# Merge gates and branch products of a hybrid decoder block computed with their columns over the partitions

## The chip, the cores and the metric

The kernel runs on one core of a Trainium2 chip. The time is that of one execution on the device, in microseconds (us). The engines are named as in the profile: PE is the matrix engine TensorE, PEld its weight loads, DVE is VectorE, ACT is ScalarE, POOL is GpSimd and SP is SyncE, which issues nearly all transfers from device memory.

## The reference

One decoder block, 256 tokens (S) of 2048 features (D), float32. Two token mixers work on projections of the same normalised input. Each result is gated and projected by its own branch matrix; the two branch products are merged by sigmoid gates, and the merged matrix is projected out.

```python
proj = h @ w_in                                     # 2048 x 11824
(qa, kc, vc, ks, vs, kw, vw, ga, za, qb, kb, vb, zb, ma, mb) = jnp.split(proj, IN_SPLITS, axis=-1)
...
ya = (oa * jax.nn.silu(za.astype(F32))).astype(x.dtype) @ w_br_a      # 1024 x 2048
yb = (ob * jax.nn.silu(zb.astype(F32))).astype(x.dtype) @ w_br_b      # 1024 x 2048
merged = jax.nn.sigmoid(ma) * ya + jax.nn.sigmoid(mb) * yb
out = merged @ w_out                                                  # 2048 x 2048
return x + (gate[:, None, :] * rms_norm(out, g_post)).astype(x.dtype)
```

`ma`, `mb`, `ya`, `yb` and `merged` are 256 x 2048. `gate`, like the scale and shift inside `h`, is a third of `c @ w_ada + b_ada`, a product of one row.

## The kernel before, in words

**Weights.** Every weight matrix is read once, in tiles of 1024 columns per partition (`raw`, seven buffers): for the large products two blocks of 128 rows by a panel of 512 columns. `prep` (L473) splits a tile into two parts: ACT rounds it to `wH` (L477), and DVE subtracts to get the rest, `wL` (L479). For the branch and output products POOL takes every fourth item of the list instead of DVE, where that item is a weight tile (L478). There are three buffers each for `wH` and `wL`, and conversion runs three items ahead of the products. The activations are split in the same way (`xH`, `xL`; `yH`, `yL`; `mH`, `mL`), and a product is the sum of three: H x H, L x H and H x L.

**Products.** `product` (L518) has two forms. In the ordinary one the activations are the stationary operand, 128 tokens of them, and 512 weight columns move (L535, L536 with `wH`, L538 with `wL`): the result has tokens over the partitions, `job.ps[t]` is the token half t. In the other one (`job.turned`) 128 weight columns are stationary and the activations of all 256 tokens move (L525, L527, L530): the result has columns over the partitions, and `job.ps[t]` holds the column blocks 2t and 2t+1 of the panel, 256 tokens of each. Only `za` and `zb` use it before the change.

**Order.** The list `items` (L410 to L454) holds the weight tiles in the order of their transfers and products. The panels of w_in are taken in passes over row ranges as parts of `h` become ready; partial results are collected in SBUF, those of `ma` in `MA`. The last pass ends with `mb`. Then come the branch products `br`, four column panels p, for each panel branch a (four tiles) and then branch b (four tiles), and at the end the output product, four panels of eight tiles. Between the branch tiles stand 32 tiles of `w_ada`, the gate's third. DVE multiplies each by its part of `c` and adds it to `gacc` (L497 for the first of a half, L499 for the others); they need no PE. The main loop (from L1158) lets the side generators make a step, evacuates finished products, prepares what is due and issues the products of one item. Each engine works through its own queue in the order that results from this.

**Evacuation and merge.** When the product of branch a and panel p is complete, DVE forms (MA + 1) x product (L619), since `MA` holds tanh(ma/2). For branch b it does the same with `MB` (L619) and adds the two (L622), for each t; the panel is then "merged". The generator `side_main` (L1084 to L1101) takes it up: for each token half t it issues four PE transposes into the PSUM tile `m_ps` (L1090), so that columns lie over the partitions, as the last product needs. ACT writes half of that to `mH` (L1096) and DVE the rest to `mL` (L1097), in pieces that don't cross the boundaries of `groups`, (0,1), (1,3), (3,7), (7,10), (10,13), (13,16) in blocks of 128 columns. After the second half it notes "mT" of the panel, for which the output product asks (L567).

Of the kernel before, what the change touches and what calls it, by code (L numbers as in the profile page):

```python
# [9 lines left out]
F32 = mybir.dt.float32  # L10
# [3 lines left out]
AF = mybir.ActivationFunctionType  # L14
OP = mybir.AluOpType
# [5 lines left out]
NT = S // 128  # L21
# [25 lines left out]
def _build(ctx, tc, x, c, positions, w_ada, b_ada, g_pre, g_post, w_in, pe_ck, pe_cv, w_ck1, w_ck2,  # L47
           w_cv1, w_cv2, w_br_a, w_br_b, w_out, out):
    nc = tc.nc
    V, A, T, G, DMA = nc.vector, nc.scalar, nc.tensor, nc.gpsimd, nc.sync  # L50
# [4 lines left out]
    psum = ctx.enter_context(tc.tile_pool(name="psum", bufs=1, space=PSUM))  # L55
# [7 lines left out]
    ident = const.tile([128, 128], F32)  # L63
# [75 lines left out]
    class Parts:  # L139


        def __init__(self):
            self.at = {}
# [181 lines left out]
    MA = big.tile([128, NT, D], F32, name="MA", tag="ma")  # L325
# [30 lines left out]
    done = set()  # L356
# [5 lines left out]
    class Job:  # L362


        def __init__(self, n, first, last, srcT, key):
            self.n, self.kt0, self.kt1, self.srcT, self.key, self.ps = n, first, last, srcT, key, None

            self.turned = key[0] == "proj" and key[3][0] in ("za", "zb")

    def w_item(w, kt0, nk, c0, jobs):  # L370
        it = Item()
# [38 lines left out]
    a, b = PASSES[0]  # L410
# [6 lines left out]
    a, b = PASSES[1]  # L417
# [3 lines left out]
    a, b = PASSES[2]  # L421
# [4 lines left out]
    a, b = PASSES[3]  # L426
# [251 lines left out]
    def side_main():  # L678
# [35 lines left out]
        for which in range(2):  # L714
            off = 256 * which
            ps = psum.tile([128, NT, 2, 128], F32, name="kc_ps", tag="pt")
# [3 lines left out]
            for a in range(2):  # L720
                KC = work.tile([128, 2, 256], F32, name="KC", tag="P", bufs=3)
                for t in range(NT):
                    lo = slice(0, 127) if t == 0 else slice(127, 255)
                    for b in range(2):
                        src = ps[64 * b:64 * (b + 1), t, a]
# [10 lines left out]
                dH, dL = (BS[:, which, :, l, 2 * a:2 * a + 2] for l in range(2))  # L736
# [6 lines left out]
        for which in range(2):  # L743
# [12 lines left out]
            ps = psum.tile([128, 2, 64], F32, name="hidT_ps", tag="pv")  # L756
# [5 lines left out]
            if which == 0:  # L762
                ps = psum.tile([64, 64], F32, name="kc2_ps", tag="pv")
# [8 lines left out]
                ps = psum.tile([128, 64], F32, name="kcT_ps", tag="pv")  # L772
# [6 lines left out]
            else:  # L779
                VBD = const.tile([128, 2, 8, 64], F32)  # L780
                ps = psum.tile([128, 2, 64], F32, name="vc2_ps", tag="pv")
# [201 lines left out]
        ps = psum.tile([128, NT, 2, 128], F32, name="pcT_ps", tag="pt")  # L983
# [6 lines left out]
        for cb in range(0, 8, 2):  # L990
            pr = cb // 4
            ps = psum.tile([128, 2, NT, 128], F32, name="oc_ps", tag="pv")
# [11 lines left out]
        for t in range(NT):  # L1004
            for X, tag in ((QB, "pt"), (KB, "pv")):
                for hh in range(2):
                    ps = psum.tile([128, 512], F32, name="b_ps", tag="pt" if hh == 0 else "pv")
                    for j in range(4):
                        o = hh * 512 + j * 128
# [49 lines left out]
        for br, (O, Z, tags, key) in enumerate(((QA, ZA, ("kb", "vb"), "za"), (QB, ZB, ("qa", "za"), "zb"))):  # L1059
# [7 lines left out]
            for cb in range(0, 8, 2):  # L1067
# [4 lines left out]
                dH, dL = (y[:, cb:cb + 2, :].rearrange("p b s -> p (b s)") for y in (yH, yL))  # L1072
# [7 lines left out]
        mH, mL = Parts(), big.tile([128, KT, S], F32R, name="mL", tag="xH")  # L1080
# [3 lines left out]
        for p in range(4):  # L1084
            while ("merged", p) not in done:
                yield
            for t in range(NT):
                ps = psum.tile([128, 4, 128], F32, name="m_ps", tag="pt")
                for j in range(4):
                    T.transpose(ps[:, j, :], MA[:, t, (4 * p + j) * 128:(4 * p + j + 1) * 128], ident)  # L1090
                ts = slice(t * 128, (t + 1) * 128)
                for a, b in groups:
                    a, b = max(a, 4 * p), min(b, 4 * p + 4)
                    if a < b:
                        dH, o = mH.at[a]
                        A.activation(dH[:, a - o:b - o, ts], ps[:, a - 4 * p:b - 4 * p], AF.Copy, scale=0.5)  # L1096
                        V.scalar_tensor_tensor(mL[:, a:b, ts], ps[:, a - 4 * p:b - 4 * p], 0.5,  # L1097
                                               dH[:, a - o:b - o, ts].bitcast(F32), op0=OP.mult, op1=OP.subtract)
                if t == NT - 1:
                    done.add(("mT", p))  # L1100
                yield  # L1101

        fin["o"] = big.tile([128, NT, D], F32, name="og", tag="mb")
        fin["x"] = big.tile([128, NT, D], F32, name="xr", tag="ma")
# [10 lines left out]
        for half in range(2):  # L1115
# [5 lines left out]
            for n in range(2):  # L1121
                ps = psum.tile([128, 512], F32, name="g_ps", tag="pv")
# [6 lines left out]
        done.add("G")  # L1129

    side.append(side_main())

    def side_step(must=False):
# [40 lines left out]
    for t in range(NT):  # L1174
# [5 lines left out]
        for p in range(4):  # L1180
            sl = slice(p * 512, (p + 1) * 512)
            o, xr = fin["o"][:, t, sl], fin["x"][:, t, sl]
# [27 lines left out]
```

## Time and profile before

| | |
|---|---|
| median of 3 runs | 841.33 us (840.12 to 841.64) |
| the profiled execution: its own time | 840.99 us |
| its span in the trace | 839.2 us |
| mean granted clock of PE | 0.993 |
| PE matmuls of 512 columns of activations by wL (`L538`, yH) | 128, 40.7 us busy, 398 ns mean |
| POOL's own wL operations (`L479 POOL`) | 15, 37.6 us busy, 2510 ns mean |
| DVE's gate steps (`L499` into gacc) | 30, 43.9 us busy, 1464 ns mean |

The span runs from the first to the last record of the profiled execution, and the run's own time contains a little more. Busy times of PE add up durations of matmuls that overlap in its pipeline, so one matmul's duration (398 ns) is longer than the distance between the starts of two that follow each other. A row of a timeline gives start, duration, engine, line, operation, output and inputs, and in brackets how long the engine had been idle before it and who released it. In a row of grouped instructions the figures behind the bar are busy time, mean, and idle time before them with its releaser.

### The profile page before, as it was taken

How to read it: one execution, taken by the hardware profiler on the slowest of the kernel's cores; microseconds unless marked ns; L12 is line 12 of the kernel's file. 1: busy time of each engine (PE TensorE's matmuls, PEld its weight loads, DVE VectorE, ACT ScalarE, POOL GpSimd, SP SyncE). 2: the span in 40 equal slices, each digit the busy share in tenths (PEclk: the TensorE clock that was granted, in tenths of full speed). 3: DMA queues.
4: the chain of work that ended last, by engine and by line, in shares of the span. 5: the costliest groups of instructions: out<-in, count | busy, mean ns of one | idle time of the engine just before them, and what ended most of it. 6: DMA issues, size and time to landing. Idle time of an engine off the chain costs nothing.

```text
span 839.2 us, 12023 instructions
## 1 busy us (share of the span) xinstructions
PE 800.3 (95%) x4200; PEld 672.1 (80%) x4200; DVE 695.1 (83%) x1080; ACT 416.4 (50%) x671; POOL 135.6 (16%) x128
## 2 busy tenths in 40 slices
PE   5997999999999999999999999999999989999995
PEld 4785778889887778888888999888888868888884
DVE  4999999999997888898978998777676998855335
ACT  3953263343434446575766666445544433444452
POOL 4200000000000025154311110001003032122221
PEclk9999999999999999999999999999999999999998
DMA  9988899999798547844444545554589989986622
GB/s 313 369 295 262 246 311 291 366 301 325 253 337 295 160 154 227 261 137 128 137 138 116 141 134 158 170 154 145 151 292 322 338 281 324 302 294 196 191 93 100
DMA packets 106663, 193.27 MB, mean 230 GB/s; under 512 B 7561, under 2 KB 36073, under 8 KB 105961
## 3 DMA queue, kind: packets, MB, share of 16 engines
q1 hardware_dynamic: 105088, 189.17, 69.7%
q10 hardware_dynamic: 1514, 3.33, 1.2%
q8 instruction: 33, 0.54, 0.3%
q14 instruction: 28, 0.23, 0.1%
HBM read 190.38 MB, written 2.10 MB: 229 GB/s over the span
## 4 chain that ended last, share of the span: by engine, by line
PE 51%; DVE 4%; issue 1%; ACT 1%; DMA 1%; DVEq 0%; ACTq 0%
PE mm L535 13%; PE mm L536 13%; PE mm L538 13%; PE mm L530 2%; PE mm L525 2%; PE mm L527 2%; DVE wL L479 1%; PE pt_ps L901 1%; PE sA L865 1%; DVE og L1187 1%; PE pvb_ps L1035 1%; PE sB L1025 1%; PE ot_ps L925 1%; PE ot_ps L923 1%; DMA raw<-in_w_ada_dram 1%
## 5 line engine op out<-in xcount | busy, mean ns | idle before, releaser
L477 ACT ACTIVATE wH<-raw 128x1024 fp32r<-128x1024 f32 (+2 forms) x276 | 275.9, 1002 | 326.3 <-PE mm L536 184.0
L479 DVE TENSOR_TENSOR wL<-raw,wH 128x1024 fp32r<-128x1024 f32 (+2 forms) x261 | 309.4, 1191 | 82.9 <-ACT wH L477 80.4
L535 PE MATMUL mm<-wH,xH 128*128 128x512 f32 (+2 forms) x640 | 247.5, 390 | 8.7 <-DVE KB L608 2.5
L536 PE MATMUL mm<-wH,xL 128*128 128x512 f32 (+2 forms) x640 | 245.7, 386 | 0.0
L538 PE MATMUL mm<-wL,xH 128*128 128x512 f32 (+2 forms) x640 | 198.5, 387 | 0.7 <-DVE wL L479 0.6
L535 PEld LDWEIGHTS mm<-wH,xH 128*128 128x128 f32 x640 | 120.2, 188 | 35.1 <-issue 6.1
L538 PEld LDWEIGHTS mm<-wL,xH 128*128 128x128 f32 x640 | 117.7, 188 | 27.7 <-DVE wL L479 2.8
L536 PEld LDWEIGHTS mm<-wH,xL 128*128 128x128 f32 x640 | 120.4, 188 | 23.4 <-DVE xL L237 0.5
L499 DVE SCALAR_TENSOR_TENSOR ST<-raw,vecT,ST 128x768 f32<-128x768 f32 (+2 forms) x75 | 76.3, 1017 | 0.3
L525 PE MATMUL mm<-xH,wH 128*128 128x256 f32 x256 | 67.5, 284 | 1.2 <-DVE VB L608 1.2
L527 PE MATMUL mm<-xL,wH 128*128 128x256 f32 x256 | 66.9, 280 | 0.0
L479 POOL TENSOR_TENSOR wL<-raw,wH 128x1024 fp32r<-128x1024 f32 x15 | 37.6, 2510 | 130.9 <-ACT wH L477 130.9
L530 PE MATMUL mm<-xH,wL 128*128 128x256 f32 x256 | 53.6, 282 | 0.4 <-DVE wL L479 0.4
L535 PE MATMUL mm<-wH,yH 128*128 128x512 f32 x128 | 51.2, 400 | 0.0
L536 PE MATMUL mm<-wH,yL 128*128 128x512 f32 x128 | 51.0, 399 | 0.0
L536 PE MATMUL mm<-wH,mL 128*128 128x512 f32 x128 | 50.8, 397 | 0.0
L535 PE MATMUL mm<-wH,mH 128*128 128x512 f32 x128 | 50.7, 396 | 0.0
L499 DVE SCALAR_TENSOR_TENSOR gacc<-raw,vecT,gacc 128x1024 f32<-128x1024 f32 x30 | 43.9, 1464 | 7.5 <-DMA raw<-in_w_ada_dram 7.4
L525 PEld LDWEIGHTS mm<-xH,wH 128*128 128x128 f32 x256 | 48.0, 188 | 1.9 <-ACT wH L477 1.0
L527 PEld LDWEIGHTS mm<-xL,wH 128*128 128x128 f32 x256 | 48.2, 188 | 0.0
L530 PEld LDWEIGHTS mm<-xH,wL 128*128 128x128 f32 x256 | 40.1, 189 | 1.0 <-DVE wL L479 1.0
L538 PE MATMUL mm<-wL,yH 128*128 128x512 f32 x128 | 40.7, 398 | 0.0
(294 smaller groups left out, 1010.2 us busy)
## 6 DMA issues: line engine op xcount, KB each, us to landing
raw<-in_w_in_dram SPq DMA_DIRECT2D x165, 512.0 KB, 4.4
raw<-in_w_ada_dram SPq DMA_DIRECT2D x48, 512.0 KB, 5.3
raw<-in_w_ada_dram SPq DMA_DIRECT2D x48, 384.0 KB, 4.6
raw<-in_w_out_dram SPq DMA_DIRECT2D x32, 512.0 KB, 4.9
raw<-in_w_br_a_dram SPq DMA_DIRECT2D x16, 512.0 KB, 5.6
raw<-in_w_br_b_dram SPq DMA_DIRECT2D x16, 512.0 KB, 5.4
raw<-in_w_in_dram SPq DMA_DIRECT2D x29, 256.0 KB, 3.0
raw<-in_w_ada_dram SPq DMA_DIRECT2D x24, 256.0 KB, 6.0
```

Source lines behind the costliest of these rows:

```text
L477: A.activation(H, raw, AF.Copy)
L479: (G if on_pool else V).tensor_tensor(L, raw, H.bitcast(F32), op=OP.subtract)
L499: V.scalar_tensor_tensor(acc, r, cc, acc, op0=OP.mult, op1=OP.add)
L525: T.matmul(ps, lhsT=it.H[:, j, bs], rhs=sH[:, it.kt0 + j, :], start=(first and j == 0 and b == 0), stop=False, skip_group_check=True)
L527: T.matmul(ps, lhsT=it.H[:, j, bs], rhs=sL[:, it.kt0 + j, :], start=False, stop=False, skip_group_check=True)
L530: T.matmul(ps, lhsT=it.L[:, j, bs], rhs=sH[:, it.kt0 + j, :], start=False, stop=(last and j == it.nk - 1), skip_group_check=True)
L535: T.matmul(ps, lhsT=sH[:, it.kt0 + j, ts], rhs=it.H[:, j, cs], start=(first and j == 0), stop=False)
L536: T.matmul(ps, lhsT=sL[:, it.kt0 + j, ts], rhs=it.H[:, j, cs], start=False, stop=False)
L538: T.matmul(ps, lhsT=sH[:, it.kt0 + j, ts], rhs=it.L[:, j, cs], start=False, stop=(last and j == it.nk - 1))
L865: T.matmul(o, lhsT=QT[:, u.t, h // 2, h % 2, :], rhs=KTt[:, hl, :, 0:128] if u.t == 0 else KTt[:, hl, u.br, :], start=(hl == 0), stop=(hl ...
L901: T.transpose(ps[:, j, :], u.P[:, j * 128:(j + 1) * 128], ident)
L923: T.matmul(ps, lhsT=vr.rearrange("p l d -> p (l d)"), rhs=u.H[:, :, b, :], start=(first and b == 0), stop=False, skip_group_check=True)
```

## The change

The turned form is used for the `ma` and `mb` panels and for both branch products as well. `MA` and `MB` then hold at `[:, t, p*512:(p+1)*512]` the column blocks 4p+2t and 4p+2t+1 with 256 tokens each. Everything between is elementwise and stays as it is. The merged panel has its columns over the partitions already, so the transposes and `m_ps` go, and ACT and DVE read `MA` from SBUF. One generator step handles both t of a panel.

```diff
-            self.turned = key[0] == "proj" and key[3][0] in ("za", "zb")
+            self.turned = key[0] == "br" or key[0] == "proj" and key[3][0] in ("za", "zb", "ma", "mb")
...
             for t in range(NT):
-                ps = psum.tile([128, 4, 128], F32, name="m_ps", tag="pt")
-                for j in range(4):
-                    T.transpose(ps[:, j, :], MA[:, t, (4 * p + j) * 128:(4 * p + j + 1) * 128], ident)
-                ts = slice(t * 128, (t + 1) * 128)
+                k0 = 4 * p + 2 * t
+                src = MA[:, t, p * 512:(p + 1) * 512].rearrange("p (b s) -> p b s", b=2)
                 for a, b in groups:
-                    a, b = max(a, 4 * p), min(b, 4 * p + 4)
+                    a, b = max(a, k0), min(b, k0 + 2)
                     if a < b:
                         dH, o = mH.at[a]
-                        A.activation(dH[:, a - o:b - o, ts], ps[:, a - 4 * p:b - 4 * p], AF.Copy, scale=0.5)
-                        V.scalar_tensor_tensor(mL[:, a:b, ts], ps[:, a - 4 * p:b - 4 * p], 0.5,
-                                               dH[:, a - o:b - o, ts].bitcast(F32), op0=OP.mult, op1=OP.subtract)
-                if t == NT - 1:
-                    done.add(("mT", p))
-                yield
+                        A.activation(dH[:, a - o:b - o], src[:, a - k0:b - k0], AF.Copy, scale=0.5)
+                        V.scalar_tensor_tensor(mL[:, a:b], src[:, a - k0:b - k0], 0.5, dH[:, a - o:b - o].bitcast(F32),
+                                               op0=OP.mult, op1=OP.subtract)
+            done.add(("mT", p))
+            yield
```

In the changed file L1094 and L1095 are what L1096 and L1097 were, and lines up to L1089 keep their numbers. The orders below show queues as the two programs have them; a row is a line, an operation, its output and inputs, and the shape, with a count where equal ones follow each other.

First piece: DVE in the branch stage, where the second half of the gate begins (L497) and branch a of panel 1 is evacuated (MA by L619). Before:

```order
L479 TENSOR_TENSOR wL<-raw,wH 128x1024
L1097 SCALAR_TENSOR_TENSOR mL<-m_ps,mH_6752 128x128
L619 SCALAR_TENSOR_TENSOR MA<-MA,mm 128x512 x2
L479 TENSOR_TENSOR wL<-raw,wH 128x1024
L497 TENSOR_SCALAR gacc_6886<-raw,vecT 128x1024
L499 SCALAR_TENSOR_TENSOR gacc_6886<-raw,vecT,gacc_6886 128x1024 x2
L479 TENSOR_TENSOR wL<-raw,wH 128x1024
```

And now:

```order
L497 TENSOR_SCALAR gacc_7796<-raw,vecT 128x1024
L479 TENSOR_TENSOR wL<-raw,wH 128x1024
L619 SCALAR_TENSOR_TENSOR MA<-MA,mm 128x512
L499 SCALAR_TENSOR_TENSOR gacc_7796<-raw,vecT,gacc_7796 128x1024
L619 SCALAR_TENSOR_TENSOR MA<-MA,mm 128x512
L479 TENSOR_TENSOR wL<-raw,wH 128x1024
L499 SCALAR_TENSOR_TENSOR gacc_7796<-raw,vecT,gacc_7796 128x1024 x2
L479 TENSOR_TENSOR wL<-raw,wH 128x1024
```

The second wL of the first listing is the second of the other, too: it stood ahead of the first two gate steps of this half, and now stands behind them. The next wL has four gate steps of the half ahead of it where it had three.

Second piece: DVE directly behind the first, where branch b of panel 1 is evacuated (MB by L619), merged (L622) and converted (mL). Before:

```order
L499 SCALAR_TENSOR_TENSOR gacc_6886<-raw,vecT,gacc_6886 128x1024
L619 SCALAR_TENSOR_TENSOR MB<-MB,mm 128x512
L499 SCALAR_TENSOR_TENSOR gacc_6886<-raw,vecT,gacc_6886 128x1024
L622 TENSOR_TENSOR MA<-MA,MB 128x512
L619 SCALAR_TENSOR_TENSOR MB<-MB,mm 128x512
L479 TENSOR_TENSOR wL<-raw,wH 128x1024
L622 TENSOR_TENSOR MA<-MA,MB 128x512
L1097 SCALAR_TENSOR_TENSOR mL<-m_ps,mH_6752 128x3x128
```

And now:

```order
L499 SCALAR_TENSOR_TENSOR gacc_7796<-raw,vecT,gacc_7796 128x1024
L619 SCALAR_TENSOR_TENSOR MB<-MB,mm 128x512
L622 TENSOR_TENSOR MA<-MA,MB 128x512
L499 SCALAR_TENSOR_TENSOR gacc_7796<-raw,vecT,gacc_7796 128x1024
L619 SCALAR_TENSOR_TENSOR MB<-MB,mm 128x512
L1095 SCALAR_TENSOR_TENSOR mL<-MA,mH_7616 128x512
L622 TENSOR_TENSOR MA<-MA,MB 128x512
L479 TENSOR_TENSOR wL<-raw,wH 128x1024
```

The first merge step moved ahead of a gate step, and the wL moved behind the first mL and the second merge step.

Third piece: ACT at the conversion of the same panel. Before:

```order
L477 ACTIVATE wH<-raw 128x1024 x5
L1096 ACTIVATE mH_6752<-m_ps 128x3x128
L477 ACTIVATE wH<-raw 128x1024
L1096 ACTIVATE mH_6753<-m_ps 128x128
L477 ACTIVATE wH<-raw 128x1024
```

And now:

```order
L477 ACTIVATE wH<-raw 128x1024 x7
L1094 ACTIVATE mH_7616<-MA 128x512
L477 ACTIVATE wH<-raw 128x1024
L1094 ACTIVATE mH_7616<-MA 128x256
L1094 ACTIVATE mH_7617<-MA 128x256
```

The same wH follows the first mH of the panel in both; that mH now waits for DVE's L622 where it waited for the transposes. The queues of SP and POOL are the same in both programs. PE's has the transposes no longer, and two matmuls of 256 columns for each of 512 in the four products named.

## The prediction

> **What bounds the kernel now.** I began with the page: busy times, then the chain of work that ended last.
>
> ```profile
> span 839.2 us, 12023 instructions
> PE 800.3 (95%) x4200; PEld 672.1 (80%) x4200; DVE 695.1 (83%) x1080; ACT 416.4 (50%) x671; POOL 135.6 (16%) x128
> PE 51%; DVE 4%; issue 1%; ACT 1%; DMA 1%; DVEq 0%; ACTq 0%
> ```
>
> TensorE (PE) works in 95% of the span, and most of the chain that the profile could follow is PE. A matmul more or less is therefore worth its full start-to-start time, unless PE waits there anyway. The next two views are the windows of PE alone (length, PE busy with the instructions started or running, granted clock, DMA share, GB/s) and of all engines (PE, PEld, DVE, ACT, POOL, then the same).
>
> ```profile
> 182.04:204.54 22.50, 22.50 (x192) 1.00 0.98 322
> 183.00:203.00 20.00, 20.00 (x172) 1.00 0.97 315
> 604.44:664.11 59.67, 59.67 (x259) 1.00 0.90 311
> 691.32:694.78 3.46, 3.46 (x11) 0.52 0.99 353
> ...
> 640.00:664.00 24.00, 24.00 (x106) 19.63 (x105) 19.71 (x18) 10.05 (x10) 5.23 (x2) 1.00 0.95 335
> 664.00:688.00 24.00, 23.23 (x105) 18.38 (x103) 23.86 (x23) 10.22 (x14) 8.27 (x3) 1.00 0.81 275
> 688.00:712.00 24.00, 21.07 (x89) 17.20 (x90) 21.75 (x23) 8.55 (x11) 4.94 (x2) 0.93 0.91 332
> ```
>
> In the stage of the branch products PE is full until 664 us. Between 664 and 712 VectorE (DVE) is nearly full as well (23.86 and 21.75 of 24 us), and PE falls short. So a term on PE alone can be worth less there than its length: once PE runs ahead, DVE sets the pace. What PE waited for, in the whole span, and its timeline around the longest of these waits:
>
> ```profile
> PE m_ps L1090 <- DVE MA L622: 3.7, 1, 3.7
> PE mm L535 <- DVE QB L610: 1.7, 1, 1.7
> ...
> 686.61 0.61 PE L538 MATMUL mm<-wL,yH 128*128 128x512 f32 x2
> 690.93 0.63 PE L1090 MATMUL m_ps<-ident,MA 128*128 128x128 f32 x4 [3.71 <-DVE MA L622]
> 691.32 0.68 PE L535 MATMUL mm<-wH,yH 128*128 128x512 f32 x1
> 694.78 0.42 PE L535 MATMUL mm<-wH,yH 128*128 128x512 f32 x1
> ```
>
> The transposes for the second column panel stand in PE's queue ahead of matmuls that need nothing from them, and hold these up until the merge of L622 is done.
>
> **What the change removes.** All of it is on PE.
>
> ```profile
> 664.50 0.44 PE m_ps L1090 x4
> 697.03 0.44 PE m_ps L1090 x4
> ...
> L1090 PE MATMUL m_ps<-ident,MA 128*128 128x128 f32 x32 | 4.9, 275 | 3.8 <-DVE MA L622 3.7
> ```
>
> The 32 transposes stand in 8 groups of 4. The chain puts a group at 0.44 us, first and last of them alike: 8 x 0.44 = **3.5 us**. The wait at 687: the pair that starts at 686.61 occupies PE for two starts of 0.231 us (pace below), to 687.07; the transposes start at 690.93, so **3.9 us** are idle. After it the clock is halved: from 691.32 to 694.78 eight 512-column matmuls start in 3.46 us where full clock needs 8 x 0.231 = 1.85, which is **1.6 us** lost to a granted clock of 0.52. Together 9.0 us.
>
> **What it adds in matmuls.** 384 matmuls of 512 columns each for ma, mb and the branches, 1152 in all, become 2304 of 256. The za/zb products run in the new form already: the window from 182.04 holds 191 starts and one begun before, 22.50 / 191 = 117.8 ns. The old form: 59.67 / 258 = 231.3 ns. A pair costs 2 x 117.8 - 231.3 = 4.3 ns more, times 1152 = **+5.0 us**. Bounds: with 20.00 / 171 = 117.0 ns (the row from 183) the pair costs 2.7 ns, +3.1 us; with the old form at 24.00 / 105 = 228.6 ns (the row from 640) 7.0 ns, +8.1 us. I take the two longest stretches, where one start more or less weighs least.
>
> The Trainium skill, "TensorE: Matmul & The Clock Gate", section "Wait — 56ns, not 53.3ns?", gives a warm matmul its columns at 2.4 GHz plus about 2.5 ns whatever their number. By that rule the split would cost 1152 x 2.5 ns = 2.9 us (an estimate from that page) and the sum below would be 2.1 us lower; the trace speaks for more (4.3 ns), and both its forms are slower than the page's 215.7 ns at 512.
>
> **The conversions of the merged output.** They go from 18 pairs to 12, read from SBUF instead of PSUM.
>
> ```profile
> L1097 DVE SCALAR_TENSOR_TENSOR mL<-m_ps,mH 128x128 fp32r<-128x128 f32 (+2 forms) x18 | 7.0, 388 | 2.7 <-ACT mH L1096 2.6
> L1096 ACT ACTIVATE mH<-m_ps 128x128 fp32r<-128x128 f32 (+2 forms) x18 | 6.4, 355 | 13.9 <-PE m_ps L1090 9.9 <-DVE mL L1097 3.9
> L1074 DVE SCALAR_TENSOR_TENSOR yL<-ZB,yH x4: 683/684/686, 609.5 to 611.3; 128x512 fp32r<-128x512 f32 x4
> L1073 ACT ACTIVATE yH<-ZB x4: 613/632/632, 590.2 to 608.5; 128x512 fp32r<-128x512 f32 x4
> ```
>
> The same operations from SBUF cost 0.68 us on DVE and 0.63 on ScalarE (ACT) for 512 columns; eight of 256 (about 0.42, the 388 ns mean being of mixed sizes) and four of 512 make 6.1 us against 7.0 on DVE. The amounts are as before, off PE's path and hidden by its matmuls; what counts is where one stands.
>
> **The wait that takes the stall's place.** Without the transposes PE runs on until it lacks a wL. These are the rows of DVE, POOL and ACT there.
>
> ```profile
> 684.98 3.42 DVE L499 SCALAR_TENSOR_TENSOR gacc<-raw,vecT,gacc 128x1024 f32<-128x1024 f32 x1
> 688.32 0.68 DVE L619 SCALAR_TENSOR_TENSOR MB<-MB,mm 128x512 f32<-128x512 f32 x1
> 688.91 1.27 DVE L499 SCALAR_TENSOR_TENSOR gacc<-raw,vecT,gacc 128x1024 f32<-128x1024 f32 x1
> 690.11 0.68 DVE L622 TENSOR_TENSOR MA<-MA,MB 128x512 f32<-128x512 f32 x1
> 690.71 0.67 DVE L619 SCALAR_TENSOR_TENSOR MB<-MB,mm 128x512 f32<-128x512 f32 x1
> 691.31 1.21 DVE L479 TENSOR_TENSOR wL<-raw,wH 128x1024 fp32r<-128x1024 f32 x1
> ...
> 683.85 3.46 POOL L479 TENSOR_TENSOR wL<-raw,wH 128x1024 fp32r<-128x1024 f32 x1 [3.12 <-ACT wH L477]
> 694.50 2.53 POOL L479 TENSOR_TENSOR wL<-raw,wH 128x1024 fp32r<-128x1024 f32 x1 [7.20 <-ACT wH L477]
> ...
> 693.31 1.06 ACT L477 ACTIVATE wH<-raw 128x1024 fp32r<-128x1024 f32 x1 [1.22 <-PE mm L536]
> ```
>
> *When PE wants it.* The wL of 691.31 belongs to the second weight tile after the stall. From 687.07 PE has twelve matmuls left of the stalled tile (1.41 us), 24 of the next (2.83) and four of the tile itself (0.47) before its first use of wL: 691.8. Two groups of transposes, both of panel 0, no longer stand before 687: 0.9 less, 690.9.
>
> *When it is ready.* In the new DVE order (second piece above) one merge step and one mL of 512 columns, 0.60 us each from start to start, stand ahead of this wL that stood behind it: it ends near 692.52 + 1.2 = 693.7. That alone is a wait of 2.8 us. POOL may add to it. The new order lets ACT convert the first half of the merged panel at about 689.6 (the first L622 moves ahead of a gate), then the next wH (1.06) from 690.2 to 691.3, two microseconds earlier than its 693.31, since the buffer that it waited for is no longer held by the stalled PE. POOL follows 0.13 us behind that wH, as at 694.50, hence at 691.4, before the wL. What two such operations do to each other stands in the rows: POOL's from 683.85 took 3.46 us with DVE's wL beside it, and DVE's gate behind it 3.42 instead of 1.27, while at 688.32 a step that reads PSUM took its usual 0.68. So POOL's 2.4 us would come ahead of the wL: ready at 696.1, a wait of 5.2.
>
> The Trainium skill, "SBUF — State Buffer", section "Who interferes with whom", says that a DVE instruction with two SBUF inputs shuts out a GpSimd one that reads SBUF, and the other way round, and that the order of issue decides. By that rule the new mL (MA and mH, both SBUF) can be held up where the old one, from PSUM, could not; the 3.42 us agrees, and no row of this kernel shows such an mL beside POOL.
>
> Bounds 2.8 and 5.2 (and nothing at all, if DVE comes earlier). I take **+4.4 us**: POOL first is likelier, but rests on a few tenths. Part of it may be waited for earlier:
>
> ```profile
> 677.24 1.22 DVE L479 TENSOR_TENSOR wL<-raw,wH 128x1024 fp32r<-128x1024 f32 x1
> 681.06 0.63 PE L538 MATMUL mm<-wL,yH 128*128 128x512 f32 x2
> ...
> DVE gacc L499 <- DMA raw<-in_w_ada_dram: 7.4, 9, 2.7
> ```
>
> Two gate steps of 1.2 us now stand ahead of this wL (first piece above), ready at 678.46 before and at 680.9 now; PE wants it at 681.06 - 0.46 (four matmuls of 256 before the first use instead of four of 512) - 0.9 = 679.7: 1.2 us. That isn't added, since it moves PE's later need back by as much. It does split the 4.4 into 1.2 and 3.2. The clock stayed at full speed in the stages with waits up to 1.7 and fell after 3.9; it then stayed low for 3.46 us, which I read as the length that it looks at. 3.2 is under that, so I take no clock cost, bounds 0 to 1.6. The other gates that move ahead by one wL meet transfers that come late (at most 2.7 us), against a slack of the wL of 681.06 - 678.46 = 2.6 and the like: 0, bounds 0 to +1. Behind the waiting matmul in PE's queue are only branch tiles; the steps of L619 and the next wH buffers wait for them, and so the next transfers. SP's and POOL's own orders don't change.
>
> **The sum**, against the profiled run's own 840.99 us (span 839.2 and 1.8 around it): 840.99 - 9.0 + 5.0 + 4.4 = **841.4**, beside a median of 841.33 of the runs shown: no change that can be told. A measurement of this kernel tells about 0.2% (1.7 us) from no change, so faster means under 839.65 and slower over 843.0.
>
> **Rivals.**
> - *The wait is short* (chance 0.22): POOL's operation comes behind the wL, 2.8 us or less, with no wait at the other end: 837.0 to 839.8. For it: the queues settle within tenths. Against: the freed wH buffer lets ACT, and with it POOL, go two microseconds sooner.
> - *The long wait comes in one piece* (0.22), the slower one: POOL holds DVE off the wL, PE idles 5.2 us at that matmul and the clock halves behind it, 1.6 us more: 840.99 - 9.0 + 5.0 + 6.8 = 843.8. It decides from an idle stretch of about 3.5 us on. For it: 3.9 did so at 691.32. Against: an earlier wait takes its share.
> - *The split is dear* (0.06): 8.1 instead of 5.0: 844.5.
> - *The split is cheap* (0.05): 3.1 us by the lower row: 839.5; the page on TensorE named above comes to nearly the same.
>
> The forecast itself, 839.7 to 843.0, has 0.45. Faster: 0.22 and 0.05, 0.27; slower: 0.22 and 0.06, 0.28; same 0.45. The range from 838.0 to 844.0 leaves out half of the short-wait case and part of the two dear ones, about 2 in 10.
>
> **What would show it.** Matmuls: 4200 + 1152 - 32 = 5320 less missing records; in long stretches 118 ns from start to start, in the ma panels early on too. The wait of m_ps on MA gone, and a new one of L530 on wL L479, 3 to 4 us, near 690, with a smaller one of about 1 us some ten microseconds before. A POOL wL between the first L622 of panel 1 and the wL that PE lacks. PEclk 1.00 from 680 to 710. I would be wrong in the wait if PE stays full from 664 to 712, in the clock if a window behind the wait shows 0.5, and in the pace if whole windows of ma or mb run above 120 or below 117 ns.

## The result, and the profile after

The changed kernel takes 852.4 us (median of five runs, 848.5 to 855.9) against 841.5; the ratio is 1.0128, 95% interval 1.0091 to 1.0165. A sixth run fell in a slower state (983.7 us, granted clock 0.754) and is left out. The forecast was 841.4 with a range to 844.0: it was wrong, and on the slow side. The profile is that of a run of 855.0 us. Three lines of its page (span, busy times, chain):

```profile
span 853.2 us, 14232 instructions
PE 805.0 (94%) x5320; PEld 728.3 (85%) x5320; DVE 699.8 (82%) x1074; ACT 415.1 (49%) x665; POOL 135.2 (16%) x128
PE 43%; DVE 7%; DMA 5%; issue 1%; ACT 0%; DVEq 0%; SPq 0%
```

The 5320 matmuls are as counted. PE is busy for 4.7 us more, but the span is 14.0 us longer, so two thirds of the loss are idle time; and in the chain DVE and the transfers (DMA) have grown from 4% and 1% to 7% and 5%. What PE waited for, and the windows of all engines in the branch stage, columns as before:

```profile
PE mm L530 <- DVE wL L479: 9.7, 7, 3.2
PE mm L538 <- DVE wL L479: 2.9, 4, 2.3
...
640.00:664.00 24.00, 22.36 (x189) 22.15 (x188) 18.20 (x12) 9.46 (x10) 8.90 (x3) 1.00 0.86 287
664.00:688.00 24.00, 21.49 (x166) 21.08 (x165) 20.25 (x22) 8.01 (x12) 2.77 (x1) 0.93 0.83 281
688.00:712.00 24.00, 19.23 (x154) 18.82 (x153) 22.60 (x20) 8.13 (x10) 8.05 (x4) 0.95 0.81 280
```

The wait of the transposes is gone, and 12.6 us of waits for wL stand where there were 1.0. PE now falls short from 640 on, not only behind 664, and in the first window no engine is full: DVE works 18.2 of 24 us. DVE itself waits, and its waits tell for what. Its rows (total, times, longest), whole span:

```profile
DVE gacc L499 <- DMA raw<-in_w_ada_dram: 16.9, 14, 3.3
DVE ST L499 <- DMA raw<-in_w_ada_dram: 3.6, 4, 1.8
```

Before, gate steps waited 7.4 us for their transfers. How that reaches PE is seen in the timelines of DVE, POOL and PE at the start of the branch stage (here and below, rows in between are left out):

```profile
647.27 1.29 DVE L499 SCALAR_TENSOR_TENSOR gacc<-raw,vecT,gacc 128x1024 f32<-128x1024 f32 x1 [0.85 <-DMA raw<-in_w_ada_dram]
648.47 3.42 DVE L479 TENSOR_TENSOR wL<-raw,wH 128x1024 fp32r<-128x1024 f32 x1
653.74 1.28 DVE L499 SCALAR_TENSOR_TENSOR gacc<-raw,vecT,gacc 128x1024 f32<-128x1024 f32 x1 [1.85 <-DMA raw<-in_w_ada_dram]
654.95 1.22 DVE L479 TENSOR_TENSOR wL<-raw,wH 128x1024 fp32r<-128x1024 f32 x1
...
647.90 2.92 POOL L479 TENSOR_TENSOR wL<-raw,wH 128x1024 fp32r<-128x1024 f32 x1 [2.56 <-ACT wH L477]
...
651.95 0.50 PE L530 MATMUL mm<-yH,wL 128*128 128x256 f32 x2 [1.64 <-DVE wL L479]
```

A gate step waits at the head of DVE's queue; the wL behind it starts at 648.47, just late enough to meet POOL's work from 647.90, takes 3.42 us instead of 1.22, and PE waits for it until 651.95. The same happens far ahead of the branch products, with a step for the scale and shift (ST) in an early pass:

```profile
145.23 1.02 DVE L499 SCALAR_TENSOR_TENSOR ST<-raw,vecT,ST 128x768 f32<-128x768 f32 x1 [1.84 <-DMA raw<-in_w_ada_dram]
146.77 1.48 DVE L479 TENSOR_TENSOR wL<-raw,wH 128x608 fp32r<-128x608 f32 x2
147.60 0.55 PE L538 MATMUL mm<-wL,xH 128*128 128x304 f32 x2 [2.30 <-DVE wL L479]
```

That place uses products in the old form (L538): not the form of the product, but a place in DVE's queue is at work. The third place is the one of the forecast, the merge of panel 1:

```profile
705.84 2.67 DVE L1095 SCALAR_TENSOR_TENSOR mL<-MA,mH 128x512 fp32r<-128x512 f32 x1
708.44 0.68 DVE L622 TENSOR_TENSOR MA<-MA,MB 128x512 f32<-128x512 f32 x1
709.04 1.21 DVE L479 TENSOR_TENSOR wL<-raw,wH 128x1024 fp32r<-128x1024 f32 x1
...
705.59 2.38 POOL L479 TENSOR_TENSOR wL<-raw,wH 128x1024 fp32r<-128x1024 f32 x1 [4.15 <-ACT wH L477]
...
710.30 0.80 PE L530 MATMUL mm<-yH,wL 128*128 128x256 f32 x2 [3.20 <-DVE wL L479]
```

There it went as worked out: POOL's wL comes first, the mL from SBUF takes 2.67 us beside it, and PE waits 3.2 us. So the theory for the experiments: **order**, the steps on tiles of w_ada that moved ahead of a wL. By the two orders of DVE's queue these are 48 of the 112 (28 of the 80 early ones, 20 of the 32 gate steps), most of them by one wL, some by two to four. Its rival: **form**, the turned products run PE into late weights whatever the order.

### The profile page after: what moved, and what is told of

The parts are those of the page before. It is cut to its first block, busy times and chain, and to the rows that moved or that the text cites. A ratio compares the mean times of both kernels' runs of the same rounds, so it can differ in the third digit from the quotient of the medians.

```text
span 853.2 us, 14232 instructions
## 1 busy us (share of the span) xinstructions
PE 805.0 (94%) x5320; PEld 728.3 (85%) x5320; DVE 699.8 (82%) x1074; ACT 415.1 (49%) x665; POOL 135.2 (16%) x128
## 4 chain that ended last, share of the span: by engine, by line
PE 43%; DVE 7%; DMA 5%; issue 1%; ACT 0%; DVEq 0%; SPq 0%
PE mm L530 7%; PE mm L525 7%; PE mm L527 7%; PE mm L535 5%; PE mm L536 5%; PE mm L538 5%; DMA raw<-in_w_ada_dram 5%; DVE wL L479 2%; PE pt_ps L901 1%; DVE gacc L499 1%; PE sA L865 1%; DMA raw<-in_w_in_dram 1%; DVE og L1184 1%; PE pvb_ps L1035 1%; PE sB L1025 1%
## 5 line engine op out<-in xcount | busy, mean ns | idle before, releaser
L525 PE MATMUL mm<-xH,wH 128*128 128x256 f32 x768 | 202.6, 285 | 1.2 <-DVE VB L608 1.2
L527 PE MATMUL mm<-xL,wH 128*128 128x256 f32 x768 | 199.7, 280 | 0.0
L530 PE MATMUL mm<-xH,wL 128*128 128x256 f32 x768 | 158.4, 282 | 0.8 <-DVE wL L479 0.8
L535 PE MATMUL mm<-wH,xH 128*128 128x512 f32 (+2 forms) x384 | 144.7, 382 | 8.8 <-DVE KB L608 2.5
L525 PEld LDWEIGHTS mm<-xH,wH 128*128 128x128 f32 x768 | 144.2, 188 | 2.0 <-ACT wH L477 1.0
L527 PEld LDWEIGHTS mm<-xL,wH 128*128 128x128 f32 x768 | 144.5, 188 | 0.1
L536 PE MATMUL mm<-wH,xL 128*128 128x512 f32 (+2 forms) x384 | 144.4, 379 | 0.0
L530 PEld LDWEIGHTS mm<-xH,wL 128*128 128x128 f32 x768 | 119.4, 189 | 1.6 <-DVE wL L479 1.6
L538 PE MATMUL mm<-wL,xH 128*128 128x512 f32 (+2 forms) x384 | 117.3, 381 | 3.0 <-DVE wL L479 2.9
L538 PEld LDWEIGHTS mm<-wL,xH 128*128 128x128 f32 x384 | 69.6, 188 | 18.9 <-DVE wL L479 5.6
L525 PE MATMUL mm<-yH,wH 128*128 128x256 f32 x256 | 68.8, 289 | 0.0
L499 DVE SCALAR_TENSOR_TENSOR gacc<-raw,vecT,gacc 128x1024 f32<-128x1024 f32 x30 | 42.5, 1415 | 17.0 <-DMA raw<-in_w_ada_dram 16.9
```

The costliest lines, as they stand in the source:

```text
L499: V.scalar_tensor_tensor(acc, r, cc, acc, op0=OP.mult, op1=OP.add)
L525: T.matmul(ps, lhsT=it.H[:, j, bs], rhs=sH[:, it.kt0 + j, :], start=(first and j == 0 and b == 0), stop=False, skip_group_check=True)
L527: T.matmul(ps, lhsT=it.H[:, j, bs], rhs=sL[:, it.kt0 + j, :], start=False, stop=False, skip_group_check=True)
L530: T.matmul(ps, lhsT=it.L[:, j, bs], rhs=sH[:, it.kt0 + j, :], start=False, stop=(last and j == it.nk - 1), skip_group_check=True)
L535: T.matmul(ps, lhsT=sH[:, it.kt0 + j, ts], rhs=it.H[:, j, cs], start=(first and j == 0), stop=False)
L536: T.matmul(ps, lhsT=sL[:, it.kt0 + j, ts], rhs=it.H[:, j, cs], start=False, stop=False)
```

## The experiments

All times are medians; each run is compared with the kernel before on its own chip. The medians of the kernel before run from 840.7 to 841.6 us from chip to chip, so differences of about 1 us between runs tell nothing. The column "branch stage" is from the first to the last matmul with yL in the one trace of that run.

| run | products | steps on w_ada tiles | POOL in the branch stage | us | ratio to before (95%) | branch stage |
|---|---|---|---|---|---|---|
| before | old form | old order | 7 wL | 841.3 | | 95.8 |
| changed | turned | new order | 7 | 852.4 | 1.0128 (1.0091-1.0165) | 105.3 |
| e1 | turned | old order | 7 | 842.5 | 1.0017 (1.0005-1.0029) | 96.5 |
| e2 | turned | only the gate steps in old order | 7 | 846.0 | 1.0062 (1.0038-1.0085) | 95.9 |
| e3 | old form | new order | 7 | 844.7 | 1.0045 (1.0028-1.0062) | 96.2 |
| e4 | turned | all late | 7 | 844.6 | 1.0041 (1.0024-1.0058) | 94.1 |
| e8 | turned | old order, gate steps late | 7 | 842.1 | 1.0006 (0.9995-1.0018) | 97.3 |
| e5 | turned | old order | 5 | 837.7 | 0.9962 (0.9947-0.9977) | 91.7 |
| e6 | old form, no transposes | old order | 7 | 837.8 | 0.9963 (0.9949-0.9977) | 93.5 |
| e7 | turned, with transposes | new order | 7 | 858.0 | 1.0199 (1.0184-1.0214) | 108.7 |
| e10 | turned, wL asked for late | new order | 7 | 854.1 | 1.0165 (1.0144-1.0185) | 105.7 |
| e12 | turned, wL asked for late | as it came out | 7 | 851.4 | 1.0118 (1.0090-1.0147) | 105.2 |
| e11 | turned, wL asked for late | old order | 5 | 836.6 | 0.9954 (0.9939-0.9968) | 91.1 |
| e14 | turned | new order | 0 | 850.8 | 1.0123 (1.0102-1.0145) | 101.0 |
| e15 | turned, wL asked for late | old order | 0 | 837.9 | 0.9965 (0.9953-0.9978) | 91.8 |
| e16 | old form | old order | 0 | 837.1 | 0.9955 (0.9937-0.9972) | 91.8 |
| e17 | old form | new order | 0 | 844.2 | 1.0037 (1.0023-1.0051) | 98.6 |

**Order or form (e1, e2, e3, e4).** A table holds, for each of the 112 steps on a tile of w_ada, the number of DVE's wL behind which it is kept: taken from the order before (e1), so for the gate steps alone (e2), or the place that the list of items gives (e4). For e3 the kernel before issues a step ahead of a wL wherever the changed kernel's order has it so.

```diff
+            if not on_pool:
+                wLs.append(iL)
...
+                k = BEHIND[len(seen)]
+                seen.append(k)
+                with behind(*wLs[k - 1:k]):
                     if it.kt0 + j == 0:
```

> The changed kernel, with each DVE step on a tile of w_ada (L497, L499) kept behind the wL behind which it stood before the change. Theory (order): PE lost 2.6 us at 146 and 6.4 us between 640 and 660 because such a step, one wL earlier than before, waited for its transfer with the wL behind it; with the old order both go, and the time is 843 to 846 us. Rival (form): the turned products ask for a wL after 0.47 us instead of 0.93 and run PE into the transfers whatever the order; then 851 us or more, with waits of L530 on wL of over 8 us in all between 640 and 720.

> The kernel before, with its DVE steps on tiles of w_ada moved to the places that they have in the changed kernel, relative to the wL; nothing else is changed. Order: PE waits of 2 us or more for wL at about 146 and of 4 to 7 us in all between 640 and 660, time 848 to 851 us. Form: within 1.5 us of the kernel before, no wait of PE for wL over 1 us.

> The changed kernel with only the gate steps of the branch stage in their old places, the earlier steps as the change has them. Order: the wait at 146 stays (2.3 us), those between 640 and 660 go; 846 to 849 us. Form: 851 us or more.

> The changed kernel with every step on a tile of w_ada behind all wL of weight tiles that precede its tile in the list, mostly one or two places later than before the change. Order: no wL stands behind a late transfer; 841 to 845 us, not slower than with the old order. Form: 851 us or more. If steps that come late hold up raw buffers and so later transfers, PE waits for wL or wH behind them, and the time lies over that with the old order.

e1 gives back 9.9 of the 10.9 us: order, and the rival for the turned kernel falls. e2 splits it: the gate steps 6.4 us (852.4 - 846.0), the earlier steps 3.5 (846.0 - 842.5); by the intervals in the table each is uncertain by two to four us. One expectation for e2 failed: the wait at 146 did not stay at 2.3 us. In its trace, that of its fastest run, PE waits 0.54 us there and 1.01 at 218.87 for a transpose behind the ST steps (1.55 together), and the branch products begin 1.5 us after e1's (645.4 and 643.9). e4 shows that later still is no better: its median is 2.1 us over e1's, though the profiled run, at 841.3 us the fastest of its ten, has the shorter branch stage. e3 was a miss: the same order costs the old form only 3.3 us, where 7 to 10 were expected.

**What is left in e1 (e5, e8).** e1's PE still waits 3.8 us, at 705.58, and then runs at half clock. DVE and POOL ahead of that in e1, and PE's window behind it:

```profile
696.24 2.90 DVE L1105 SCALAR_TENSOR_TENSOR mL<-MA,mH 128x512 fp32r<-128x512 f32 x1
700.26 2.94 DVE L1105 SCALAR_TENSOR_TENSOR mL<-MA,mH 128x256 fp32r<-128x256 f32 x2
704.32 1.21 DVE L484 TENSOR_TENSOR wL<-raw,wH 128x1024 fp32r<-128x1024 f32 x1
...
695.74 2.85 POOL L484 TENSOR_TENSOR wL<-raw,wH 128x1024 fp32r<-128x1024 f32 x1 [5.48 <-DVE wL L484]
699.80 2.77 POOL L484 TENSOR_TENSOR wL<-raw,wH 128x1024 fp32r<-128x1024 f32 x1 [1.22 <-ACT wH L482]
...
705.58:709.00 3.42, 3.42 (x17) 0.54 0.82 241
```

e5 gives those two wL to DVE; e8 puts e4's late gate steps beside e1's early ones.

```diff
-            on_pool = it.kind == "w" and it.jobs[0].key[0] != "proj" and i % 4 == 0
+            on_pool = it.kind == "w" and it.jobs[0].key[0] != "proj" and i % 4 == 0 and i not in (324, 328)
```

> The changed kernel with the old order of steps and wL (as e1), and the two wL that POOL worked on beside the mL of panel 1 given to DVE instead. In e1 PE still waited 3.8 us at about 702 and then ran at half clock, behind mL steps that took 2.9 us each beside POOL's wL. Theory (POOL and an mL from SBUF shut each other out): the mL take 0.7 us again, the wait shrinks below 1.5 us and the half clock goes; 837 to 839.5 us. Rival (DVE simply has too much to do there, whoever does those wL): the wait stays at 3 us or more, 841 us or more.

> The changed kernel with the early steps in their old order and the gate steps of the branch stage behind every wL that precedes them in the list. Order theory: no gate step can hold up a wL by a late transfer; if that is worth something beyond the old order, 840 to 842 us, else as e1, 842 to 843.5 us. If late steps hold up raw buffers, over 844 us.

In e5 the mL of 512 columns takes 0.68 us (timeline of DVE), PE's waits for wL in the whole span are 1.5 us, and the clock stays full in the window that had 0.93 before:

```profile
694.31 0.68 DVE L1105 SCALAR_TENSOR_TENSOR mL<-MA,mH 128x512 fp32r<-128x512 f32 x1
PE mm L540 <- DVE wL L484: 1.5, 3, 0.7
688.00:712.00 24.00, 23.30 (x197) 23.10 (x196) 23.61 (x24) 9.81 (x12) 1.65 (x1) 1.00 0.94 331
```

DVE works 23.6 of 24 us, more than in the kernel before, and PE is nearly full. So it wasn't too much work, but the two engines shutting each other out. e8 is as e1: once the gate steps no longer hold up a wL, moving them further back gives nothing. What e4 loses against e1 therefore most likely lies with the early steps, which e4 moved back and e8 did not.

**Transposes apart from the form (e6, e7).** e6 takes the new merge into the kernel before, so that it leaves out the transposes that its products need; e7 takes the old merge into the changed one, which transposes what should stay as it is. Both compute something else and serve for the time alone.

```diff
-                ps = psum.tile([128, 4, 128], F32, name="m_ps", tag="pt")
-                for j in range(4):
-                    T.transpose(ps[:, j, :], MA[:, t, (4 * p + j) * 128:(4 * p + j + 1) * 128], ident)
+                src = MA[:, t, p * 512:(p + 1) * 512].rearrange("p (b s) -> p b s", b=2)
```

> The kernel before with its products in the old form and its old order, but with the transposes left out: the merged matrix goes to the last product as it lies in MA, read from SBUF, so that the computation is another one. It prices what the removal of transposes and stall brings by itself, without the new form. If the new wait for wL (as in e1) comes with the merge from SBUF: 837.5 to 840.5 us. If it comes from the turned form alone, the whole 9 us are gained: 831 to 834 us.

> The changed kernel's products and its new order of steps and wL, with the old merge put back (32 transposes through PSUM, of a matrix that has no need of them, so that the computation is another one). Beside e3 (old form, same order, 844.7 us) it tells what the turned form does to the waits. If the form (a wL asked for 0.46 us earlier) turns e3's short waits into long ones: 850 us or more, with 5 us or more of waits for wL between 640 and 665. If form and waits are independent: e3 and the matmuls' 2.9 us, 846.5 to 849 us, waits as in e3.

e6: of the 9.0 us that transposes and stall were worth, 841.6 - 837.8 = 3.8 arrive. The rest went where the forecast said, in the old form as well: PE's waits in the branch stage of e6, the half clock behind the longer one (3.63 x 0.43 = 1.6 us lost), and its mL there, again beside a wL of POOL's (from 691.10, 2.53 us).

```profile
PE mm L557 <- DVE wL L488: 4.1, 2, 3.1
...
695.37:699.00 3.63, 3.63 (x10) 0.57 0.70 216
...
691.32 2.86 DVE L1114 SCALAR_TENSOR_TENSOR mL<-MA,mH 128x512 fp32r<-128x512 f32 x1
```

e7's time is over 850, but between 640 and 665 PE waits for wL once, 2.3 us and not 5, and for the transposes 7.1 us in the branch stage: the time came out as expected, the reason only in part.

**Why the same order is dearer in the changed kernel (e10, e12, e14, e16, e17).** e10 and e12 let PE ask for a wL after eight matmuls of 256 instead of four:

```diff
+            at = []
             for b in range(2):
...
+                at.append((b, job.ps[t][:, b * S:(b + 1) * S], slice(c0, c0 + 128)))
+            for b, ps, bs in at:
                 for j in range(it.nk):
                     T.matmul(ps, lhsT=it.H[:, j, bs], rhs=sH[:, it.kt0 + j, :], start=(first and j == 0 and b == 0),
...
+            for b, ps, bs in at:
                 for j in range(it.nk):
                     T.matmul(ps, lhsT=it.L[:, j, bs], rhs=sH[:, it.kt0 + j, :], start=False,
```

> The changed kernel with its own order of steps and wL held fast, but each turned product first does the eight wH matmuls of a pair of column blocks and then the four with wL, so that PE asks for a wL after 0.94 us as in the old form, not after 0.47. Theory (the earlier demand turns short lateness into waits): as e3 with the matmuls' 2.9 us, 846 to 849 us, and waits for wL under 1.5 us in all between 640 and 665. Rival (it is something else of the turned form, or that order alone): 851 us or more, with waits there as in the changed kernel (3.7 us).

> The changed kernel with wL asked for later as the only edit; the order of steps and wL is what comes out, still mostly one place early. Theory as for e10: 843 to 849 us. Rival: as the changed kernel, 850 us or more.

> e5 (old order, two wL taken from POOL) with wL asked for later, as in e10. e5 had 1.5 us of waits of L530 for wL left, and 837.7 us. If these go with the later demand: 836 to 837.2 us; if nothing changes, 837.2 to 838.5.

The theory of the earlier demand falls: e10 is as slow as the changed kernel and e12 nearly so, and e10's waits for wL in the branch stage are 12.6 us (8.9 there in the changed kernel). e11, e5 with that edit, has the lowest median of all and is faster than both kernels; its ratio and e5's have overlapping intervals, so what the edit adds to e5 is open.

> The changed kernel with its own order of steps and wL held, and all seven branch wL of POOL given to DVE. Theory (a gate step that comes late by its transfer pushes the next wL or gate into POOL's work, which shuts it out for two more microseconds, and that makes the following transfers later still): without POOL's work the waits for wL between 640 and 720 fall under 4 us, 843 to 847 us. Rival (late transfers alone keep the loop going): 850 us or more, waits as in the changed kernel (8.9 us).

> e11 with all seven branch wL on DVE instead of five on POOL. If what POOL's work costs by shutting DVE out is more than DVE's 1.2 us for each: 834.5 to 836.3 us. If DVE becomes too full: 837 us or more.

> The kernel before, in its own order, with the seven branch wL on DVE: how much of the gain of e5 and e15 has nothing to do with the change. If POOL's shutting out delayed the merge at 690 as the rows of that stage suggest, the wait of the transposes (3.7 us) and the half clock shrink: 836 to 839 us. If not: 840.5 us or more.

> The kernel before with the new order of steps and wL (as e3) and the seven branch wL on DVE (as e16): the fourth corner beside e14 (turned, new order, no POOL, 850.8 us), e15 (turned, old order, 837.9) and e16 (old form, old order, 837.1). If the new order is dear only in the turned form, whatever POOL does: 838 to 841.5 us, as e16 and up to 4 us more. If e3 was cheap only because POOL's work happened to miss the late steps: 846 us or more, near e14.

These four take POOL out of the stage (the list in the edit of e5 is then 288, 292, 296, 316, 320, 324, 328). DVE's waits for gate transfers, in the order e16 (old form, old order), e17 (old form, new order), e14 (turned, new order), and then PE's waits in the branch stage of e3 (two lines) and of e16:

```profile
DVE gacc L509 <- DMA raw<-in_w_ada_dram: 4.5, 7, 1.1
...
DVE gacc L523 <- DMA raw<-in_w_ada_dram: 17.8, 13, 3.6
...
DVE gacc L523 <- DMA raw<-in_w_ada_dram: 20.2, 15, 3.0
...
PE mm L557 <- DVE wL L488: 3.1, 4, 1.1
PE m_ps L1109 <- DVE MA L641: 1.4, 1, 1.4
...
PE m_ps L1100 <- DVE MA L632: 1.1, 1, 1.1
```

e16 came out as expected, e17 between its two expectations. Without POOL the new order costs the old form 844.2 - 837.1 = 7.1 us (e17, e16) and the turned form 850.8 - 837.9 = 12.9 (e14, e15, which has the later wL as well); in the branch stage of the traces it is 6.8 and 9.2. So the order is dear in both forms, and in the old form dearer than the 3.3 us of e3. The lines of e3 show what set its price off in the branch stage: its PE waits 3.1 us for wL, but its wait for the merge is 1.4 us where the kernel before waited 3.7 and then lost 1.6 to the half clock; behind e3's the clock stays at 1.00. In e16 that wait is only 1.1 us before the order is changed, and in e17 nothing is set off. That e14 keeps 850.8 us shows that late transfers suffice: against the changed kernel (852.4, ratios 1.0123 and 1.0128) no share of POOL's can be told, and the theory that its work keeps the loop going falls. e15 missed its range: the last five wL taken from POOL bring nothing beyond e11. The 5.8 us (12.9 - 7.1) by which the new order is dearer in the turned form I could not put down to one cause; by e10 it is not the earlier demand for wL.

How the lateness keeps itself going stands in e1 and the changed kernel side by side. The tile of the second weight item of the first branch product holds its raw buffer from the start of its wH to the end of its wL for 2.9 us in e1 and for 8.0 us in the changed kernel (643.93 to the end of the wL of 648.47), since its wL stands behind a gate step that waits. SP issues the transfer of the tenth gate tile 0.03 us after that end, 8.0 us after the start of that wH; in e1 it comes 4.2 us after the start of the same wH (640.88). SP's rows, the changed kernel first, and the step that this transfer serves in the changed kernel:

```profile
651.92 0.34 SPq L467 DMA_DIRECT2D raw<-in_w_ada_dram  x1
...
645.04 0.41 SPq L471 DMA_DIRECT2D raw<-in_w_ada_dram  x1
...
657.24 2.27 DVE L499 SCALAR_TENSOR_TENSOR gacc<-raw,vecT,gacc 128x1024 f32<-128x1024 f32 x1 [1.07 <-DMA raw<-in_w_ada_dram]
```

This is one turn of the loop. That such turns add up to the whole loss is argued from DVE's waits for gate transfers (16.9 us against 7.7 in e1) and not shown turn by turn.

## Why the prediction was wrong, point by point

- **The step that failed** is "The other gates that move ahead by one wL meet transfers that come late (at most 2.7 us), against a slack of the wL of 681.06 - 678.46 = 2.6 and the like: 0, bounds 0 to +1." It measured 6.4 us for the gate steps (changed kernel less e2); in the traces (runs of 855.0 and 844.2 us) the branch stage is 105.3 us against 95.9. Nor did all move by one wL: of the 20 that moved, three did so by two or three. The slack of a wL was taken as if every lateness were new; but a late step holds its own buffer and, as at 651.92, that of the weight tile behind it, so later transfers start later. That the slack is so used up once and not refilled is my reading of it.
- A second omission beside it: only the gate steps were priced. The steps of the early passes moved in the same way and cost 3.5 us (e2 less e1). In the trace of the changed kernel the branch products begin 3.0 us after e1's (646.9 and 643.9), behind waits of 2.30 us at 147.60 and 0.94 at 220.24 that e1 does not have. The order before and now showed it; the prediction read it at the branch stage alone.
- The wait in the stall's place was right in mechanism and, once the order is put back, near in size. e1 waits 3.8 us at one matmul (4.4 forecast), behind mL steps that POOL's wL hold up; e5 takes these two wL from POOL, and 0.7 us of waiting are left in the branch stage. With the half clock behind it (3.42 x 0.46 = 1.6 us lost) e1 comes near the forecast's rival of one long wait (5.2 and 1.6). What was off is the clock: "3.2 is under that, so I take no clock cost". In the changed kernel it halved behind that very wait of 3.2 us, and behind one of 2.0 before. PE's row and windows there (length, busy, clock, DMA share, GB/s):

```profile
668.53 0.68 PE L530 MATMUL mm<-yH,wL 128*128 128x256 f32 x2 [2.04 <-DVE wL L479]
668.53:671.99 3.46, 3.46 (x16) 0.52 0.66 206
710.30:717.00 6.70, 6.70 (x33) 0.54 0.80 262
```

  What is missing from full clock there is 3.46 x 0.48 + 6.70 x 0.46 = 4.7 us, a cost that the forecast had at nothing (the 1.6 us of the kernel before are in its 9.0). It follows from the waits and is part of the price of the order, not an addition to it.

- The price of the split, +5.0 us, was about right. A clean stretch of turned products in the changed kernel (its row is x341, with 338 starts from its first to its last) and one in e1 (746 starts):

```profile
610.17:650.03 39.86, 39.86 (x341) 1.00 0.82 276
607.11:695.49 88.38, 88.38 (x749) 1.00 0.89 305
```

  That is 117.9 and 118.5 ns, against 117.8 assumed, or 5.2 to 6.5 us for the 1152 pairs. The traces agree: when the branch products begin, 768 of the 1152 pairs are done, which at 4.3 ns makes 3.3 us, and e1 is there 643.9 - 640.7 = 3.2 us behind the kernel before. The Trainium skill's rule, in "TensorE: Matmul & The Clock Gate", section "Wait — 56ns, not 53.3ns?", gives 768 x 2.5 ns = 1.9 us (an estimate from that page). The trace agrees better with 4.3 ns, though moved instructions may be part of the 3.2.
- What the change removes, 9.0 us, was right as a sum: neither the transposes nor their stall are in the trace. That much of it would be given back in new waits was right too (in e6 3.8 us remain).
- The sum without the failed steps: e1, the changed kernel in the old order, has 842.5 us, where the prediction had 841.4. That is 1.1 us more, hardly above what can be told; the half clock in e1, 1.6 us that the sum left out, would account for it.
- The gain of e5 isn't the change's: e16, the kernel before without POOL's branch wL, has 837.1. With the queues put right the two forms are equal within what can be told (e11 836.6, e15 837.9).

## What to carry to other kernels

An instruction that waits for a transfer is dear by what stands behind it in its engine's queue. Where a change lets a scheduler move such instructions, compare the two orders over the whole program, count the moves, and price them as a loop: late step, late release of its buffer, late next transfer. And price a change of order in the kernel that it will run in: in the old form it cost 3.3 us where a stall set part of it off, and 7.1 where that stall was gone. Before work is shared out to a second engine, see in the trace whether the two engines' operations on SBUF lengthen each other; here taking seven operations back from POOL was worth 4 us in the kernel before (e16), and the two that stood beside the mL nearly 5 in the turned one (e5 less e1).

## What the runs showed of the hardware

- An mL from SBUF (two SBUF inputs) took 2.67 to 2.90 us while POOL worked on a wL, and 0.68 without: the prediction had only a gate step and a wL as witnesses. The old mL from PSUM did not show it: one of 128 columns at 694.71 in the kernel before, beside POOL's wL of 694.50, took its usual 0.28 us.
- The clock halved behind a wait of 2.04 us (668.53, for about 3.5 us) and of 3.20 us (710.30, for about 6), where the kernel before had shown it only behind 3.9; in e6 and e1 it halved behind 3.10 and 3.79. Behind 2.30 us at 147.60 it stayed full, so the length of the wait alone does not decide:

```profile
148.00:151.00 3.00, 3.00 (x23) 1.00 0.95 312
```
